# A two-layer hybrid encoder: weights' low halves by an accumulating DMA, a spread final norm, and work moved from VectorE and GpSimd

## Chip, cores and metric

One core of a Trainium2 chip runs the kernel. The metric is the device time of one execution in microseconds. Engines are named as in the profile: PE is TensorE's matmul (PEld its weight load), DVE VectorE, ACT ScalarE, POOL GpSimd, and SP is SyncE, which here only issues DMAs.

## What is computed

Two layers over 1024 tokens of width 1024, float32 throughout:

```python
u = rmsnorm(h, ln_mix[i]) @ w_in[i]
(c_q, c_kv, k_rope, gate_a, gq, gk, gv, lr_f, lr_b, gate_g) = split_cols(u, IN_SPLITS)
y_mla = mla_branch(c_q, c_kv, k_rope, positions, ...) * silu(gate_a)
y_gla = gla_branch(gq, gk, gv, lr_f, lr_b, ...) * silu(gate_g)
h = h + concatenate([y_mla, y_gla], axis=-1) @ w_out[i]
h = h + sigmoid(rmsnorm(h, ple_norm[i]) @ w_ple_gate[i]) * (p[i] @ w_ple_proj[i])
# after both layers: rmsnorm(h, final_norm)
```

`mla_branch` norms the latents c_q and c_kv, projects them to four heads' queries, keys and values, rotates a 64-wide shared key and part of the queries by position, and does dense softmax attention. `gla_branch` is a gated linear attention, four heads, run forward and backward in chunks of 64 tokens, with a norm per head.

## The kernel before

The activations lie transposed: features on the 128 partitions, 1024 tokens along the free dimension. Precision comes from splitting: a float32 value is a rounded high half and a low half (the rest), and a product is three matmuls, high x high, low x high, high x low (`mm3`, L156 to 163). Weights are loaded in pieces of 128 partitions x 512 columns or less by `load_split` (L135): SP issues the load into `wr` (two buffers), ACT copies it rounded to `wh` (L141), POOL subtracts for `wl` (L142); `wh` and `wl` have five buffers each. There are 192 such loads. Activations are split by ACT and DVE (`split`, L127).

Each layer starts with `rstd` (L165), which sums squares over partitions by a matmul with ones and finds the reciprocal root with small DVE operations. The norm's weights are folded into the split activations, and the factor r_x per token is applied to each projection as DVE evicts it from PSUM: `in_qk` (L323, two operations of 64 partitions and two DMAs that fill the other half of each tile), `in_v` (L332, factor per partition), `in_gate` (L354), `latent_tile` (L498). `latent_norm` (L505) takes a second root for the latents. `gla_decay`, `gla_state` and `gla_out` (L364, L405, L469) are the linear attention: chains of ACT exponentials, DVE scans and products, a recurrence of small DVE operations (L451), and short matmuls. `rotary_tables` (L241) computes sines and cosines once, on 128 partitions in four blocks of tokens, and writes them to DRAM; `rotary_key` (L574) works on 32 or 64 partitions. `score_rows`, `turn` and `attend` (L651, L677, L688) are the softmax attention; POOL scales the exponentials (L670).

The strings in `ORDER` (L52) list the steps of each layer in order, a letter for the step: K, Q, V and G the projections of the linear attention, Z, S, O its decay, state and output, C and D the latents, N and M their norms, A the attention's gates, R, X, E, T the rotary parts, H the query heads, k and v keys and values, s and b scores and attention, y and w the output projection. A planner, run at build time, then orders each engine's instructions by a simulated timeline; every engine and SP's queue take theirs strictly in that order. PSUM is two tags, `mm` and `aux`, of two tiles of two banks.

At the end the last gate (L800 to 847) goes over two blocks of tokens, 736 and 288 wide (`TAIL`). In each, for eight tiles: matmuls (L820), eviction (L823), sigmoid, product with `pj` on POOL (L828, the last two of block two on DVE), sum (L830), squares (L834, L836). After the eight, `rstd` and the final scaling, four tiles on POOL (L838 and L843, `POOL_END`) and four on DVE (L845), and the stores (L847).

## Time and profile before

| | us |
|---|---|
| median of three runs | 1482.35 (1480.93 to 1482.83) |
| the profiled execution | 1483.45 |
| its span, first to last instruction | 1481.7 |
| PE busy | 1387.9 (94%) |
| DVE busy | 929.8 (63%) |
| ACT busy | 625.7 (42%) |
| POOL busy | 573.4 (39%) |
| mean granted TensorE clock | 0.975 |

Busy time is the time in which an engine executes; its complement is waiting. The page's shares are means over stages that differ, so the stages are read by stretches: 56 to 400 us is the input projections and linear attention of layer 0, 400 to 680 its softmax attention and output projection, up to 775 its gate; 775 to 1095 and 1095 to 1370 are the like stages of layer 1, and the rest is the last gate and the final norm. The HBM reads come to 82.34 MB. The granted clock is 1 for 2.4 GHz and 0.5 for 1.2 GHz.

### The profile page before, as it was taken

What the parts mean: (1) busy time and instruction counts of PE and PEld (TensorE: products, weight loads), DVE (VectorE), ACT (ScalarE), POOL (GpSimd) and SP (SyncE); (2) the same over time, 40 slices, a digit from 0 to 9 for tenths busy, and PEclk for the clock granted to TensorE, in tenths of its full rate; (3) what the DMA queues carried; (4) which work ended last, traced back from release to release, by engine and by line L of the source; (5) the groups of instructions that cost most, each with busy time, mean ns of one, the idle gap of its engine ahead of it and who ended that gap; (6) DMA issues with size and microseconds to landing.
All of it is one profiled execution on the core that took longest, in us unless ns stands there. A gap on an engine that the chain in (4) does not pass through costs nothing. (4 is left out here: it accounts for less than half of the span.)

```text
span 1481.7 us, 20880 instructions
## 1 busy us (share of the span) xinstructions
PE 1387.9 (94%) x8404; PEld 1173.7 (79%) x8404; DVE 929.8 (63%) x1244; ACT 625.7 (42%) x828; POOL 573.4 (39%) x334
## 2 busy tenths in 40 slices
PE   8999899889889999999999989989989999999994
PEld 6799678678678888878889877768777888878994
DVE  2687856688655645465557878676755664447548
ACT  6454364443344534343444444623333543235331
POOL 4542332321264545223452323222334645412564
PEclk9999999999999999999999999999999999999997
DMA  8321213112501031112432121111350021211333
GB/s 293 116 74 51 62 66 144 33 51 81 157 27 57 15 100 50 64 43 86 152 134 65 37 72 51 36 54 37 121 143 29 29 71 50 71 45 55 124 103 122
DMA packets 51296, 117.51 MB, mean 79 GB/s; under 512 B 6592, under 2 KB 11584, under 8 KB 51200
## 3 DMA queue, kind: packets, MB, share of 16 engines
q1 hardware_dynamic: 51200, 116.19, 23.9%
q8 instruction: 66, 1.08, 0.3%
q14 instruction: 30, 0.25, 0.1%
HBM read 82.34 MB, written 25.43 MB: 73 GB/s over the span
## 5 line engine op out<-in xcount | busy, mean ns | idle before, releaser
L142 POOL TENSOR_TENSOR wl<-wr,wh 128x512 fp32r<-128x512 f32 (+2 forms) x184 | 270.3, 1472 | 690.0 <-ACT wh L141 615.8
L141 ACT ACTIVATE wh<-wr 128x512 fp32r<-128x512 f32 (+2 forms) x184 | 111.4, 610 | 336.9 <-PE ps L162 217.4
L670 POOL TENSOR_SCALAR sc<-sc,sums 128x1024 f32<-128x1024 f32 x64 | 181.9, 2851 | 91.4 <-DVE sums L669 76.8
L129 DVE TENSOR_TENSOR el<-ps,eh 128x1024 fp32r<-128x1024 f32 x64 | 78.0, 1221 | 47.2 <-ACT eh L128 46.4
L668 ACT ACTIVATE sc<-ps,top 128x1024 f32<-128x1024 f32 x64 | 71.4, 1116 | 82.5 <-DVE top L666 78.5
L162 PE MATMUL ps<-xh,wh 128*128 128x512 f32 x288 | 93.7, 406 | 12.2 <-DVE gate L357 5.9
L451 DVE SCALAR_TENSOR_TENSOR s<-s,last 64x128 f32<-64x128 f32 x208 | 84.6, 407 | 32.6 <-ACT s L104 25.7
L665 DVE TENSOR_REDUCE top<-ps 128x1 f32<-128x1024 f32 x64 | 78.2, 1223 | 39.8 <-PE ps L662 39.7
L162 PE MATMUL ps<-x0h,wh 128*128 128x512 f32 x288 | 93.1, 405 | 7.3 <-DVE gate L357 3.8
L162 PE MATMUL ps<-xh,wl 128*128 128x512 f32 x288 | 92.5, 400 | 0.0
L162 PE MATMUL ps<-x0h,wl 128*128 128x512 f32 x288 | 92.2, 400 | 0.0
L162 PE MATMUL ps<-xl,wh 128*128 128x512 f32 x288 | 91.7, 398 | 0.0
L162 PE MATMUL ps<-x0l,wh 128*128 128x512 f32 x288 | 91.5, 399 | 0.0
L162 PE MATMUL ps<-yh,wh 128*128 128x512 f32 x256 | 80.7, 392 | 0.9 <-DVE h L722 0.9
L162 PE MATMUL ps<-yl,wh 128*128 128x512 f32 x256 | 79.5, 390 | 0.0
L162 PE MATMUL ps<-yh,wl 128*128 128x512 f32 x256 | 79.3, 390 | 0.0
L128 ACT ACTIVATE eh<-ps 128x1024 fp32r<-128x1024 f32 x64 | 65.3, 1022 | 31.7 <-PE ps L683 30.1
L162 PEld LDWEIGHTS ps<-xh,wh 128*128 128x128 f32 x288 | 55.3, 195 | 25.3 <-DVE gate L357 6.4
L162 PEld LDWEIGHTS ps<-x0h,wh 128*128 128x128 f32 x288 | 55.2, 194 | 19.9 <-DVE gate L357 4.3
L683 PE MATMUL ps<-ident,sc 128*128 128x128 f32 x512 | 66.2, 273 | 4.6 <-DVE ql L129 3.0
L683 PEld LDWEIGHTS ps<-ident,sc 128*128 128x128 f32 x512 | 59.2, 140 | 13.0 <-DVE ql L129 3.5
L162 PEld LDWEIGHTS ps<-x0h,wl 128*128 128x128 f32 x288 | 55.8, 194 | 12.2
(251 smaller groups left out, 3499.3 us busy)
## 6 DMA issues: line engine op xcount, KB each, us to landing
wr<-in_w_in SPq DMA_DIRECT2D x88, 256.0 KB, 2.6
wr<-in_w_gate SPq DMA_DIRECT2D x40, 256.0 KB, 2.6
projd<-po SPq DMA_DIRECT2D x16, 512.0 KB, 3.7
wr<-in_w_out SPq DMA_DIRECT2D x32, 256.0 KB, 2.6
xraw<-in_xT SPq DMA_DIRECT2D x8, 512.0 KB, 4.8
gqk<-gqk SPq DMA_DIRECT2D x16, 256.0 KB, 3.0
ygd<-o SPq DMA_DIRECT2D x8, 512.0 KB, 2.6
gad<-gate SPq DMA_DIRECT2D x8, 512.0 KB, 3.0
```

What stands on the lines that cost most here:

```text
L128: nc.scalar.activation(hi, src, AF.Copy)
L129: nc.vector.tensor_tensor(lo, src, hi.bitcast(F32), op=ALU.subtract)
L141: nc.scalar.activation(hi[:, :n], raw[:, :n], AF.Copy)
L142: on("wlo").tensor_tensor(lo[:, :n], raw[:, :n], hi[:, :n].bitcast(F32), op=ALU.subtract)
L162: nc.tensor.matmul(ps[:, c, :], lhsT=a, rhs=b[:, c * HC:(c + 1) * HC], start=(i == 0 and j == 0), stop=(i == n - 1 and j == 2))
L451: nc.vector.scalar_tensor_tensor(state(n)[rows], state(m)[rows], alpha[rows, m:m + 1], state(n)[rows], op0=ALU.mult, op1=ALU.add)
L665: nc.vector.tensor_reduce(m, flat(ps), axis=AX.X, op=ALU.max, negate=True)
L668: nc.scalar.activation(e, flat(ps), AF.Exp, bias=m, scale=SCALE, accum_out=sums[:, b:b + 1])
L670: nc.gpsimd.tensor_scalar(e, e, sums[:, b:b + 1], None, op0=ALU.mult)
L683: nc.tensor.transpose(out=ps[:, j, b * P:(b + 1) * P], in_=e[:, kt], identity=ident)
```

## The change

All of it is made together:

- `load_split`: up to the step Q0 of layer 0 as before (eight loads). Later ones: ACT writes the negative rounded copy into `wl`, and a DMA issued on POOL reads the weights a second time from DRAM and adds them to it.
- `in_qk`: one DVE operation on 128 partitions into a tile of `st` (three buffers), and four DMAs that write both halves of both tiles.
- `in_v`: four ACT copies with a scale per partition in place of a DVE product, per half.
- `latent_tile`: ACT copies the PSUM tile unscaled and squares it from PSUM; `rstd` gets `base`, the mean square of x kept from the layer's first root (`ax`), so that the second root allows for the missing factor.
- `rotary_key`: on 128 partitions in four blocks of tokens. Eight DMAs lay out the key, six DVE operations of 256 columns rotate it, one split follows, eight DMAs write it to DRAM and four read it back in its two places. The tables stay in SBUF as `sc4`.
- The end: the product with `pj` is always DVE's. The scaling of the first block is spread, one tile per step, over the second block's steps, into tiles of `st`. `POOL_END` goes: DVE scales all tiles.

```diff
-POOL_END = (0, 3, 4, 6)
...
     other = [False]
+    first = [True]
     def pick(tag):
         return {"mm": "aux", "aux": "mm"}[tag] if other[0] else tag
...
         nc.vector.scalar_tensor_tensor(lo, src, g, hi.bitcast(F32), op0=ALU.mult, op1=ALU.subtract)
     def load_split(src, n, dst=None):
         raw = wp.tile([P, HC], F32, tag="wr", name="wr", bufs=BUFS[2])
         hi, lo = dst or (wp.tile([P, HC], F32R, tag=t, name=t, bufs=BUFS[3]) for t in ("wh", "wl"))
         with tc.high_priority():
             nc.sync.dma_start(raw[:, :n], src)
         nc.scalar.activation(hi[:, :n], raw[:, :n], AF.Copy)
-        on("wlo").tensor_tensor(lo[:, :n], raw[:, :n], hi[:, :n].bitcast(F32), op=ALU.subtract)
+        if first[0]:
+            nc.gpsimd.tensor_tensor(lo[:, :n], raw[:, :n], hi[:, :n].bitcast(F32), op=ALU.subtract)
+        else:
+            nc.scalar.activation(lo[:, :n], raw[:, :n], AF.Copy, scale=-1.0)
+            nc.gpsimd.dma_start(lo[:, :n], src, accum_op=ALU.add)
         return hi, lo
     def load_w8(src, keep=False):
...
                     nc.tensor.matmul(ps[:, c, :], lhsT=a, rhs=b[:, c * HC:(c + 1) * HC],
                                      start=(i == 0 and j == 0), stop=(i == n - 1 and j == 2))
-    def rstd(acc, width, n=S, tmp=st, res=mt, col=None):
+    def rstd(acc, width, n=S, tmp=st, res=mt, col=None, ax=None, base=None):
         if isinstance(acc, tuple):
             mat, parts = ones_r.bitcast(F32), acc
...
         y = cp.tile([P, 32], F32, tag="nwy", name="nwy", bufs=2)[:, :nb]
         t = cp.tile([P, 32], F32, tag="nwt", name="nwt", bufs=2)[:, :nb]
-        nc.vector.tensor_scalar(a, r[:, :n].rearrange("p (b i) -> p b i", i=32)[:, :, 0], 0.5 / width, 0.5 * EPS,
-                                op0=ALU.mult, op1=ALU.add)
+        nc.vector.tensor_scalar(a, r[:, :n].rearrange("p (b i) -> p b i", i=32)[:, :, 0], 0.5 / width,
+                                0.0 if base is not None else 0.5 * EPS, op0=ALU.mult, op1=ALU.add)
+        if base is not None:
+            nc.vector.scalar_tensor_tensor(a, base, EPS, a, op0=ALU.mult, op1=ALU.add)
+        if ax is not None:
+            nc.vector.tensor_copy(ax, a)
         nc.vector.tensor_scalar(y.bitcast(I32), a.bitcast(I32), 1, None, op0=ALU.arith_shift_right)
         nc.vector.tensor_scalar(y.bitcast(I32), y.bitcast(I32), -1.0, float(0x5F3759DF - 2 ** 22 - 2 ** 31),
                                 op0=ALU.mult, op1=ALU.add)
...
     h1d = dram([8, P, S], "h1d")
     cosd = dram([32, S], "cosd")
     sind = dram([32, S], "sind")
+    krd = dram([DEPTH, 2, 2, 32, S], "krd")
     def ple_projection(i):
         ops = []
...
                 copy("ple", o, flat(ps))
                 nc.sync.dma_start(projd[i][g * 2 + c], o)
+    sc4 = cp.tile([P, 2, S // 4], F32, name="sc4")
     def rotary_tables():
         n = S // 4
         work = mt(name="rot")
-        kk, ang, *rs = (work[:, i * n:(i + 1) * n] for i in range(4))
+        kk, ang = (work[:, i * n:(i + 1) * n] for i in range(2))
+        rs = sc4[:, 1], sc4[:, 0]
         posi = kk.bitcast(I32)
         for b in range(4):
             nc.sync.dma_start(posi[b * 32:(b + 1) * 32], pos[:, b * n:(b + 1) * n].to_broadcast((32, n)))
...
         rc = cp.tile([P, 8], F32, tag="rc", name="rc", bufs=2)
-        r_x = rstd(sq.acc, D, col=rc)
+        ax = cp.tile([P, 32], F32, tag="ax", name="ax", bufs=2)
+        r_x = rstd(sq.acc, D, col=rc, ax=ax)
         afb = mt(name="afb").rearrange("p (d t c) -> p d t c", d=2, c=CH)
         nc.gpsimd.memset(afb, 0.0)
...
             ps = flat(in_tile(t + j, tag))
             pair = (mt(name="gqk0"), mt(name="gqk1"))
-            for o, own, other in ((pair[0], slice(0, CH), slice(CH, P)), (pair[1], slice(CH, P), slice(0, CH))):
-                nc.vector.scalar_tensor_tensor(o[own], ps[own], scale, r_x[own], op0=ALU.mult, op1=ALU.mult)
-                nc.sync.dma_start(o[other], o[own])
+            both = st(name="gqk")
+            nc.vector.scalar_tensor_tensor(both, ps, scale, r_x, op0=ALU.mult, op1=ALU.mult)
+            halves = (slice(0, CH), slice(CH, P))
+            for o, own in zip(pair, halves):
+                for half in halves:
+                    nc.sync.dma_start(o[half], both[own])
             return pair
         def in_v(pair):
...
             res = []
             for half in range(2):
                 v = mt(name="gv").rearrange("p (t c) -> p t c", c=2 * P)
-                nc.vector.tensor_tensor(v, ps[half], rc[:, half * 4:half * 4 + 4].unsqueeze(2).to_broadcast((P, 4, 2 * P)),
-                                        op=ALU.mult)
+                for t in range(4):
+                    nc.scalar.activation(v[:, t], ps[half][:, t], AF.Copy, scale=rc[:, half * 4 + t:half * 4 + t + 1])
                 res.append(v)
             return [[res[t // 4][:, t % 4, h * P:(h + 1) * P] for t in range(8)] for h in range(2)]
...
         def latent_tile(t, s2, tile=mt):
             ps = in_tile(t)
             o = tile(name="craw")
-            nc.vector.tensor_tensor(o, flat(ps), r_x, op=ALU.mult)
-            s2.add(o)
+            nc.scalar.activation(o, flat(ps), AF.Copy)
+            s2.add(flat(ps))
             return o
         def latent_norm(raws, s2, off, width):
-            r = rstd(s2.acc, width)
+            r = rstd(s2.acc, width, base=ax)
             res = []
             for j, raw in enumerate(raws):
                 nc.vector.scalar_tensor_tensor(raw, raw, gv(off, j), r, op0=ALU.mult, op1=ALU.mult)
...
         def rotary_key():
-            cos, sin = xx[2:]
-            t1, t2 = mt(name="t1"), mt(name="t2")
-            k1, k2 = slice(64, 96), slice(96, 128)
-            nc.vector.tensor_tensor(t1[0:32], small[k1], cos[k1], op=ALU.mult)
-            nc.vector.tensor_tensor(t2[0:32], small[k2], sin[k2], op=ALU.mult)
-            nc.vector.tensor_tensor(t1[32:64], small[k1], sin[k1], op=ALU.mult)
-            nc.vector.tensor_tensor(t2[32:64], small[k2], cos[k2], op=ALU.mult)
-            nc.vector.tensor_tensor(t1[0:32], t1[0:32], t2[0:32], op=ALU.subtract)
-            nc.vector.tensor_tensor(t1[32:64], t1[32:64], t2[32:64], op=ALU.add)
+            n = S // 4
+            work = mt(name="kr")
+            k1, k2, u1, u2 = (work[:, i * n:(i + 1) * n] for i in range(4))
+            rot = mt(name="krot")[:, :2 * n]
+            cos, sin = sc4[:, 0], sc4[:, 1]
+            for b in range(4):
+                for k, row in ((k1, 64), (k2, 96)):
+                    nc.sync.dma_start(k[b * 32:(b + 1) * 32], small[row:row + 32, b * n:(b + 1) * n])
+            for x1, x2, o, op in ((cos, sin, rot[:, :n], ALU.subtract), (sin, cos, rot[:, n:], ALU.add)):
+                nc.vector.tensor_tensor(u1, k1, x1, op=ALU.mult)
+                nc.vector.tensor_tensor(u2, k2, x2, op=ALU.mult)
+                nc.vector.tensor_tensor(o, u1, u2, op=op)
+            parts = mt(F32R, "krp").rearrange("p (h c) -> p h c", h=2)
+            split(parts[:, 0], parts[:, 1], rot)
             ks, kl = mt(F32R, "ks"), mt(F32R, "kl")
-            nc.scalar.activation(ks[0:64], t1[0:64], AF.Copy)
-            nc.scalar.activation(ks[64:128], t1[0:64], AF.Copy)
-            for half in (slice(0, 64), slice(64, 128)):
-                nc.vector.tensor_tensor(kl[half], t1[0:64], ks[0:64].bitcast(F32), op=ALU.subtract)
+            for i, t in enumerate((ks, kl)):
+                for b in range(4):
+                    nc.sync.dma_start(krd[L, i, :, :, b * n:(b + 1) * n].rearrange("j f n -> f j n"),
+                                      parts[b * 32:(b + 1) * 32, i].bitcast(F32).rearrange("p (j n) -> p j n", j=2))
+                for half in (slice(0, 64), slice(64, 128)):
+                    nc.sync.dma_start(t[half].bitcast(F32), krd[L, i].rearrange("j f n -> (j f) n"))
             ksl.extend((ks, kl))
         def q_head(h):
...
             u = int(w[1])
             other[0] = w.endswith("+")
             h, c = divmod(u, 2)
+            if w == "Q0":
+                first[0] = False
             if w[0].isupper():
                 step(w[0], u)
             elif w[0] == "k":
...
                 xs.append((hi, lo))
         else:
-            kept = {}
+            kept, later = {}, []
+            def finish(t, w, r, o=None):
+                hw = hs[t][:, w]
+                o = hw if o is None else o[:, :w.stop - w.start]
+                nc.vector.scalar_tensor_tensor(o, hw, vec[:, V_FIN + t:V_FIN + t + 1], r, op0=ALU.mult, op1=ALU.mult)
+                nc.sync.dma_start(outT[t][:, w], o)
             for w in TAIL:
                 n = w.stop - w.start
                 k = -(-n // HC)
...
                     nc.scalar.activation(g, g, AF.Sigmoid)
                     pj = mt(name="pj")[:, :n]
                     nc.sync.dma_start(pj, projd[L][t][:, w])
-                    eng = nc.vector if last_block and at > 5 else nc.gpsimd
-                    eng.tensor_tensor(g, g, pj, op=ALU.mult)
+                    nc.vector.tensor_tensor(g, g, pj, op=ALU.mult)
                     hw = hs[t][:, w]
                     nc.vector.tensor_tensor(hw, hw, g, op=ALU.add)
                     if at == 0:
                         nc.scalar.activation(acc, hw, AF.Square)
                     else:
                         nc.scalar.activation(g, hw, AF.Square)
-                        if at < 7:
+                        if at < 7 or not last_block:
                             nc.vector.tensor_tensor(acc, acc, g, op=ALU.add)
-                    if at in POOL_END:
-                        nc.vector.tensor_scalar(hw, hw, vec[:, V_FIN + t:V_FIN + t + 1], None, op0=ALU.mult)
-                r_f = rstd((acc, g), D, n=n)
-                for at, t in enumerate(todo):
-                    hw = hs[t][:, w]
-                    if at in POOL_END:
-                        nc.gpsimd.tensor_tensor(hw, hw, r_f[:, :n], op=ALU.mult)
-                    else:
-                        nc.vector.scalar_tensor_tensor(hw, hw, vec[:, V_FIN + t:V_FIN + t + 1], r_f[:, :n],
-                                                       op0=ALU.mult, op1=ALU.mult)
-                    nc.sync.dma_start(outT[t][:, w], hw)
+                    if later:
+                        finish(*later.pop(0), st(name="fin"))
+                if last_block:
+                    r = rstd((acc, g), D, n=n)
+                    for t in todo:
+                        finish(t, w, r[:, :n])
+                else:
+                    r = rstd(acc, D, n=n)
+                    later = [(t, w, r[:, :n]) for t in todo]
```

## Rows read from the trace of the kernel before

**Rows 1.** The page's table of busy time, share of the span, instructions

```profile
PE 1387.9 (94%) x8404; PEld 1173.7 (79%) x8404; DVE 929.8 (63%) x1244; ACT 625.7 (42%) x828; POOL 573.4 (39%) x334
```

**Rows 2.** Stretches: busy us and (x instructions) per engine, granted clock, DMA share, GB/s

```profile
56.00:400.00 344.00, 319.29 (x2336) 269.10 (x2337) 249.61 (x360) 150.50 (x202) 102.92 (x68) 0.96 0.24 78
...
775.00:1095.00 320.00, 297.99 (x2262) 252.67 (x2261) 234.42 (x341) 134.12 (x182) 93.76 (x65) 0.97 0.21 65
...
1459.60:1481.70 22.10, 3.46 (x11) 1.65 (x9) 16.01 (x40) 4.20 (x10) 5.39 (x6) 0.58 0.34 123
```

**Rows 3.** Waits of PE, 56 to 400 us: total us, times, longest

```profile
PE ps L176 <- ACT sqh L128: 6.9, 2, 4.8
PE ps L162 <- DVE gate L357: 5.3, 2, 3.8
PE ps L477 <- DVE s L451: 4.8, 1, 4.8
```

**Rows 4.** Waits of PE, 775 to 1095 us

```profile
PE ps L162 <- DVE gate L357: 7.2, 2, 5.9
...
PE ps L162 <- DVE gqk L328: 1.0, 1, 1.0
```

**Rows 5.** Groups of POOL by line, shape: xcount, busy us, mean ns

```profile
L142 POOL TENSOR_TENSOR wl<-wr,wh 128x512 fp32r<-128x512 f32 x164 | 250.0, 1528 | 604.5 <-ACT wh L141 537.8 <-issue 66.6
```

**Rows 6.** Groups of ACT by line and shape

```profile
L141 ACT ACTIVATE wh<-wr 128x512 fp32r<-128x512 f32 x164 | 101.8, 626 | 291.9 <-PE ps L162 185.4 <-issue 57.0 <-DMA wr<-in_w_in 13.0
...
L128 ACT ACTIVATE eh<-ps 128x1024 fp32r<-128x1024 f32 x64 | 65.3, 1022 | 31.7 <-PE ps L683 30.1 <-PE ps L162 1.4
```

**Rows 7.** Groups of DVE by line and shape

```profile
L328 DVE SCALAR_TENSOR_TENSOR gqk<-ps,rstd 64x1024 f32<-64x1024 f32 x16 | 19.5, 1221 | 5.7 <-PE ps L162 5.3
...
L398 DVE TENSOR_TENSOR d<-d,gqk 128x1024 f32<-128x1024 f32 x8 | 15.5, 1932 | 8.2 <-ACT d L396 8.2
...
L501 DVE TENSOR_TENSOR craw<-ps,rstd 128x1024 f32<-128x1024 f32 x10 | 12.1, 1218 | 0.2
...
L401 DVE TENSOR_TENSOR qi<-qi,gqk 128x1024 f32<-128x1024 f32 x8 | 9.8, 1225 | 6.7 <-ACT qi L395 6.7
...
L349 DVE TENSOR_TENSOR gv<-ps,rc 128x1024 f32<-128x1024 f32 x8 | 9.6, 1214 | 0.0
...
L589 DVE TENSOR_TENSOR kl<-t,ks 64x1024 fp32r<-64x1024 f32 x4 | 6.2, 1540 | 1.2 <-ACT ks L586 1.1
...
L579 DVE TENSOR_TENSOR t<-small,cos 32x1024 f32<-32x1024 f32 x2 | 2.4, 1214 | 1.9 <-DMA cos<-cosd 1.9
...
L838 DVE TENSOR_SCALAR h<-h,vec 128x736 f32<-128x736 f32 x4 | 2.4, 596 | 0.9 <-ACT acc L832 0.9
```

**Rows 8.** Timeline of DVE at the end

```profile
1450.57 9.70 DVE L845 SCALAR_TENSOR_TENSOR h<-h,vec,rstd 128x736 f32<-128x736 f32 x4
...
1466.85 0.44 DVE L823 TENSOR_TENSOR gt<-ps,rstd 128x288 f32<-128x288 f32 x1
...
1474.20 4.04 DVE L845 SCALAR_TENSOR_TENSOR h<-h,vec,rstd 128x288 f32<-128x288 f32 x4
```

**Rows 9.** Tile wl by stretches: PE, PEld and POOL instructions that touch it

```profile
56.00:400.00 344.00, 140.14 (x454) 88.09 (x454) 81.10 (x51) 0.96 0.24 78
...
775.00:1095.00 320.00, 132.51 (x430) 82.86 (x430) 70.31 (x48) 0.97 0.21 65
```

**Rows 10.** DMA issues: line, queue, xcount, KB each, median us to landing

```profile
wr<-in_w_in SPq DMA_DIRECT2D x88, 256.0 KB, 2.6
...
xraw<-in_xT SPq DMA_DIRECT2D x8, 512.0 KB, 4.8
```

**Rows 11.** Timeline of PE inside one projection: start us, us

```profile
1076.52 0.62 PE L162 MATMUL ps<-xl,wh 128*128 128x512 f32 x2
...
1082.00 0.61 PE L162 MATMUL ps<-xl,wh 128*128 128x512 f32 x2
```

**Rows 12.** Timeline of SP's queue, cosine loads of layer 1

```profile
1051.67 1.81 SPq L571 DMA_DIRECT2D cos<-cosd  x4
```

More of the change, by code (lines that the diff above doesn't have):

```diff
@@ L53 @@
          "Q0 K0 Z0 V0 S0 Z1 V1 S1 Q1 K1 Z2 G0 O0 S2 G1 Z3 G2+ C0 O1 D0 O2 S3 G3 C1 N0 D1 D2+ O3 M0 X0 A0 A1 E0 A2 k0 y2 H0 A3 T0 s0 v0 H3 k1+ s1 H1 b0 H2 s2 k2 b1 s3 y0 k3+ b2 v1 s4 y3 y1 b3 s5 b4 w0 w1+ s6 w2+ b5 w3 s7 w4 b6 w5+ s8 w6+ w7 b7")
-ENG = dict(at="V", qi="V", qb="P", og="P", gate="P", sq="V", wlo="P", kT="A", put="A", o="A", ple="A", hadd="V")
+ENG = dict(at="V", qi="V", qb="P", og="P", gate="P", sq="V", kT="A", put="A", o="A", ple="A", hadd="V")
 TCKW = {"schedule_with_timeline_sim": True}
```

## The prediction

> **What bounds the kernel now.** I read the table of the page first: PE is busy 1387.9 us of a span of 1481.7 [rows 1]. So the room is the 94 us in which PE stands still, plus what it loses at the lower clock. A table by stretches [rows 2] says where: 24.7 us idle in 56 to 400 us and 22.0 us in 775 to 1095 us (the projections and the gated linear attention of the two layers), and 18.6 us after the last projection matmul, 1459.6 us to the end. The first two stretches run at a mean granted clock of 0.96 and 0.97, and PE falls to its lower level, 1.2 GHz, after its longest idle gaps. What that costs is at most 0.04 x 319 + 0.03 x 298 = 21.7 us. The other stretches hold some 28 us of idle time, in small pieces.
>
> Next I read whom PE waited for in the two stretches [rows 3, 4]. Released by DVE: 18.1 us in 56 to 400 (seven rows; gate and s are the largest) and 18.6 us in 775 to 1095 (seven rows; gate and gqk are shown). Released by ACT: 8.3 and 2.6 us, sqh first. No row names POOL. DVE is also the busiest of the other engines there: 249.6 of 344 us and 234.4 of 320 [rows 2]. So the kernel is bound by PE, and where PE stands still DVE is usually late.
>
> **The lows of the weights.** Removed: POOL's subtraction for 184 of 192 loads (the eight before Q0 of layer 0 stay). It takes 1.53 us [rows 5]. Added: a second ACT copy, 0.63 us [rows 6], and one DMA issued on POOL, 184 x 256 KB or less.
> - POOL gives up about 270 us. PE never waited for it, so the gain is indirect. POOL's two-input operations slow DVE's: d x k takes 1.93 us where the like product with qi takes 1.23 [rows 7], and at the end DVE's final scaling takes 2.4 us for 736 columns beside POOL, where 1.23 us for 1024 columns scales to 0.89 [rows 7, 8]. Over DVE's groups in the two stretches I estimate 37 us of such excess (5.7 of it in those eight products). POOL's subtractions are 81.1 and 70.3 us there, of 102.9 and 93.8 us of POOL [rows 2, 9], so I take three quarters: DVE gets back 14 us per layer. Bounds: 0 and 18.
> - ACT pays 51 x 0.63 = 32 us and 48 x 0.63 = 30 us in the two stretches [rows 6, 9]. Elsewhere 85 more copies lie beside PE.
> - The low half now comes by a DMA that no row shows. Nearest: a plain load of the same size lands in 2.6 us, the slowest big load of the start in 4.8 [rows 10]. It moves the same bytes with a second read, so I take 5 us, 2.6 to 10. The cover is the five buffer pairs: a load feeds 24 matmuls, 5.48 us (twelve rows of two; the first of them and the one after the last are shown) [rows 11], so a load is made about four loads ahead, some 22 us. Even 10 us is hidden, and I charge nothing. Without the cover it would be a few us for each load.
> - POOL's issue of such a DMA has no row. From below it is SP's 0.45 us per issue [rows 12], from above the subtraction it replaces, 1.53 us. I take 1 us, off the path. Queued behind a waiting issue on POOL are the products of the output and the softmax scaling, as they are behind the subtraction now.
> - The raw buffer comes free after ACT's second copy, earlier than after POOL's subtraction, so SP's loads and what stands behind them in SP's queue start a little earlier. I count nothing.
>
> Against this part speaks the Trainium skill (SBUF — State Buffer, the paragraph on the "DVE blocks DMA" trap): while DVE runs a copy-like operation in its faster two-port mode, POOL cannot write the descriptors of a DMA it issues. No run here shows such a DMA. The trace shows DVE operations at twice the usual speed, but short ones: 736 columns in 0.60 us [rows 7]. By the page a DMA would start up to that much later, still inside the lead, so it would leave the sum as it is.
>
> **DVE's shorter list.** q and k: eight 128-row operations replace 16 half-height ones of 1.22 us, -9.8 us. Values: eight of 1.21 leave DVE, -9.6, and become 32 ACT copies of 256 columns, about 0.43 each by 0.63 for 512, +13.8. Latents: ten of 1.22 leave, -12.1, and become ACT copies of 1.02, +10.2; the PSUM bank is then held by two ACT reads, which matters only if ACT is late. Key: six operations of 1.2 to 1.6 us and two of 1.54, per layer, go (21.3 us over both) for six of 256 columns, about 0.35, and one of 512, about 0.7; over both layers 5.6, so -15.7; ACT saves 3. The new copies of the norm's base cost +1.2. DVE: -46 us, 23 per layer [rows 6, 7].
> Queues: SP gets 28 more issues per layer (8 for q and k, 20 for the key), 0.45 us each [rows 12], 13 us. The key's three hops in a row take 3 x 2.6 us and 5 us of work. The key is wanted only at the first scores; two gate tiles, a query head and the first keys come between, four projections of 4 to 11 us. Weight loads behind those hops have the 22 us lead. Charged: 0.
>
> **From work to time.** DVE's load in the two stretches falls by 23 + 14 = 37 us of 250 and of 234, some 15%. The 36.7 us that PE waits for DVE go by between nothing (if they are latencies of one chain) and all. I take a third, -13, since the waits are queueing behind a DVE at 73%, with chains in between. The clock returns a like share of 21.7: -7.5 (0 to -21.7). ACT gets about 86 - 3 us more in these stretches (62 + 13.8 + 10.2, less the key), going from 44% and 42% to some 56%. PE's 10.9 us of waits for ACT grow: +4 (0 to +40).
>
> **The end.** The last matmul ends at 1459.8, but its eviction starts at 1466.85, because the four final scalings of the first columns hold DVE for 9.7 us [rows 8]. From that eviction to the last scalings it is 7.35 us, and from the end of those (1474.20 + 4.04) to the end of the span 3.46 us. With DVE free at 1459.9 and eight scalings of 0.37, it would end at 1459.9 + 7.35 + 3.0 + 3.46 = 1473.7: -8. If the eight scalings of the first columns (8 x 0.89 = 7.1 us) and the products that come over from POOL (8 x 0.4) still stand in the queue, nothing is won. I take -4.
>
> Sum: -13 - 7.5 + 4 - 4 = -20.5 against the profiled execution (1483.45 us, the span and 1.75 around it). It stands 1.1 us above the median of 1482.35, so from the median: 1461.9, rounded to 1462.
>
> **Rivals.**
> - ACT takes DVE's place (slower). Place: the two stretches, where ACT is served in order and already stands with a weight copy at its head until PE frees the buffer; the exponentials and evictions queue behind two copies instead of one. Price: the part of the 83 us that lands ahead of a PE wait. It decides from 28.5 us (13 + 7.5 + 4, and the 4 of the sum), a third of it. At half: 41.5 - 24.5 = +17, 1499 us. For: 8.3 us of PE's waits are for ACT. Against: ACT remains under 60%. Chance 0.16.
> - The low halves come late. By rows: if landing plus issue exceeds the 22 us lead, each load costs a fifth of the excess, so 30 us would cost 184 x 8 / 5 = 294 us, 1776 us. It would take DVE's two-input work, and not the short fast operations alone, to hold up POOL's issues. That is the trap of the page named above, taken further than it goes. Against it: the 2.6 us row. Chance 0.04.
> - The waits are chains, not queues: DVE is relieved but PE's order and its waits stay. Then only the end gives: 1482.35 - 4 = 1478, or no change if ACT takes that too. Chance 0.16, half of it within the bound.
> - Contention was the main thing: DVE gets back all, and two thirds of waits and clock go: 36.7 x 2/3 + 21.7 x 2/3 + 6 = 45 less 4, 1441 us. It is the good end of my own case.
>
> **How the numbers follow.** My case has 0.64 (1441 to 1475), the chains 0.16, ACT 0.16, late lows 0.04. A measurement of this kernel can tell about 0.2%, 3 us, from no change. Faster: 0.64 + 0.08 = 0.72. Same 0.08. Slower 0.20. The range from 1440 to 1488 leaves out the upper part of the ACT case, the late lows and the best end of mine.
>
> **What would show it.** Right: DVE busy in 56 to 400 down from 250 to about 213 us and ACT up to about 195; the product d x k at 1.2 us; PE's waits for DVE there at 12 us; the clock at 0.97 or more; the last eviction less than 4 us after the last matmul. Wrong: PE waiting at its projections for the accumulating DMA; PE waits for ACT above 30 us; the span between the last matmul and the end still at 22 us; PE's waits for DVE unchanged though DVE's busy time fell.

## The result and the profile after

The changed kernel takes 1473.88 us (median of five runs, 1472.4 to 1477.46) against 1482.83 us for the kernel before, run beside it: ratio 0.9941 [0.9928, 0.9954]. It is 9 us faster, where 20.5 were forecast. The profiled execution spans 1470.7 us, 11.0 less than before [rows 1].

The page, busy times and the two DMA queues (packets, MB, share of 16 engines):

```profile
PE 1379.4 (94%) x8400; PEld 1168.9 (79%) x8400; DVE 819.2 (56%) x1238; ACT 737.0 (50%) x1053; POOL 427.4 (29%) x312
...
q1 hardware_dynamic: 55168, 124.05, 27.9%
q0 software_dynamic: 26496, 46.41, 18.9%
```

POOL is down from 573 to 427 us, DVE from 930 to 819, ACT up from 626 to 737 [rows 1]; q0 is the accumulating traffic on POOL's queue.

To find where the span changed, both traces are cut at the same points of PE's work: layer 0's and layer 1's first score matmul, the start of layer 1, the end of its output projection, the last gate's last matmul. The same cuts for four experiments, which are described below, stand beside them (us between cuts, each cut to within 0.8 us; the first 56 us are left out):

| stretch | before | after | e13 | e4 | e12 | e7 |
|---|---|---|---|---|---|---|
| 56 us to layer 0's first scores | 342.0 | 325.0 | 326.8 | 325.6 | 352.3 | 326.1 |
| to the start of layer 1 | 360.0 | 359.0 | 360.2 | 358.4 | 361.7 | 359.9 |
| to layer 1's first scores | 331.0 | 331.0 | 319.7 | 322.3 | 335.5 | 340.0 |
| to the end of its output projection | 275.0 | 276.6 | 276.0 | 275.9 | 275.8 | 277.9 |
| to the last gate's last matmul | 96.5 | 102.4 | 98.7 | 100.8 | 102.3 | 95.5 |
| to the end | 21.2 | 20.7 | 20.8 | 21.9 | 25.4 | 21.0 |

Layer 0 gains 17 us, the like stretch of layer 1 nothing, and the last gate loses 5.9. In after, layer 1's stretch holds 28 matmuls more than before: the whole of the first values' projection now runs ahead of the first scores, where before a part of it ran behind them. So layer 1's two stretches, to its first scores and on to the end of its output projection, are best read together: 606.0 us before, 607.6 after, 595.7 in e13. Three questions follow: what gives the 17, what takes the same gain from layer 1, and what slows the gate.

The kernel before by such cuts (columns as in [rows 2]):

```profile
56.00:398.00 342.00, 317.29 (x2327) 267.45 (x2328) 248.38 (x359) 149.45 (x200) 102.18 (x67) 0.96 0.24 77
758.00:1089.00 331.00, 309.65 (x2298) 261.58 (x2297) 242.55 (x348) 141.03 (x189) 99.02 (x67) 0.97 0.20 66
1364.00:1460.50 96.50, 95.17 (x593) 93.42 (x591) 59.30 (x71) 31.83 (x46) 55.41 (x36) 1.00 0.33 109
```

The kernel after, with the stretches of [rows 2] among them:

```profile
56.00:381.00 325.00, 310.01 (x2327) 262.89 (x2327) 199.48 (x348) 181.71 (x268) 63.36 (x66) 0.98 0.54 131
56.00:400.00 344.00, 326.66 (x2398) 276.00 (x2398) 210.22 (x364) 191.95 (x283) 76.30 (x72) 0.99 0.54 133
740.00:1071.00 331.00, 310.88 (x2326) 263.86 (x2325) 196.28 (x333) 171.84 (x257) 66.78 (x68) 0.97 0.49 115
775.00:1095.00 320.00, 292.78 (x2224) 247.10 (x2223) 188.51 (x318) 165.30 (x249) 67.03 (x63) 0.96 0.48 112
1347.60:1450.00 102.40, 96.07 (x588) 94.85 (x586) 54.25 (x88) 43.79 (x70) 17.29 (x20) 0.97 0.64 154
```

By the fixed stretches DVE is busy 210.2 and 188.5 us, ACT 192.0 and 165.3, and the clock is 0.99 and 0.96. The fixed stretch of 56 to 400 us now holds some attention, though. For equal PE work in layer 0 (2327 matmuls in either trace) DVE falls from 248.4 to 199.5, and in layer 1, with the 28 matmuls more, from 242.6 to 196.3. In layer 0 PE's idle time falls from 24.7 to 15.0 us and its busy time by 7.3 (the clock goes from 0.96 to 0.98); in layer 1 idle stays near 20 us.

Waits of PE over the whole span of after (they answer to [rows 3, 4]: total, times, longest):

```profile
PE ps L670 <- DVE ql L129: 11.1, 2, 7.1
...
PE ps L857 <- DMA wl<-in_w_gate: 5.9, 1, 5.9
PE ps L167 <- DVE afb L482: 5.8, 1, 5.8
...
PE ps L167 <- DVE gate L376: 5.2, 3, 4.6
...
PE ps L690 <- DMA qs<-rl: 5.0, 1, 5.0
PE ps L182 <- ACT sqh L128: 4.6, 3, 2.1
```

Two rows wait on DMAs that hardly mattered before (0.7 us for `qs`): `wl` in the last gate and the rotated query `qs` in layer 1.

Groups of DVE after ([rows 7] show d x k before), then the same recurrence in the kernel before:

```profile
L470 DVE SCALAR_TENSOR_TENSOR s<-s,last 64x128 f32<-64x128 f32 x208 | 78.2, 376 | 37.9 <-ACT s L102 30.8
...
L417 DVE TENSOR_TENSOR d<-d,gqk 128x1024 f32<-128x1024 f32 x8 | 12.4, 1549 | 18.2 <-ACT d L415 18.2
```

```profile
L451 DVE SCALAR_TENSOR_TENSOR s<-s,last 64x128 f32<-64x128 f32 x208 | 84.6, 407 | 32.6 <-ACT s L104 25.7
```

The recurrence, 208 operations with no change of code, went from 407 to 376 ns. d x k fell from 1.93 to 1.55 us, not to 1.23. Six of the eight products now take 1.21 to 1.23 us, four of them while POOL issues a DMA; the other two take 2.48 and 2.58 us beside POOL's product `b`, which is still there.

Groups of ACT and of POOL after [rows 5, 6], and the page's DMA issues after [rows 10]:

```profile
L146 ACT ACTIVATE wl<-wr 128x512 fp32r<-128x512 f32 x156 | 97.9, 628 | 269.3 <-PE ps L167 244.4 <-PE ps L362 11.6 <-PE ps L857 7.9
...
L369 ACT ACTIVATE gv<-ps,rc 128x256 f32<-128x256 f32 x32 | 12.7, 481 | 2.6 <-PE ps L362 2.6
...
L521 ACT ACTIVATE craw<-ps 128x1024 f32<-128x1024 f32 x10 | 10.1, 1009 | 0.0
```

```profile
L147 POOL DMA_DIRECT2D wl<-in_w_in x84 | 72.6, 870 | 354.0 <-ACT wl L146 327.5 <-ACT wh L142 13.2 <-ACT wzt L317 6.3
```

```profile
wr<-in_w_in SPq DMA_DIRECT2D x88, 256.0 KB, 3.3
wl<-in_w_in POOLq DMA_DIRECT2D x84, 256.0 KB, 4.8
...
wl<-in_w_gate POOLq DMA_DIRECT2D x32, 256.0 KB, 4.8
```

An accumulating DMA lands in 4.8 us (the medians of both groups shown) and takes POOL 0.87 us to issue; plain loads now take 3.3 us where they took 2.6.

### The profile page after: what moved, and what is told of

It reads as the page before. It is cut to its first block, busy times and chain, and to the rows that moved or that the text cites. A ratio compares the mean times of both kernels' runs of the same rounds, so it can differ in the third digit from the quotient of the medians.

```text
span 1470.7 us, 21244 instructions
## 1 busy us (share of the span) xinstructions
PE 1379.4 (94%) x8400; PEld 1168.9 (79%) x8400; DVE 819.2 (56%) x1238; ACT 737.0 (50%) x1053; POOL 427.4 (29%) x312
## 3 DMA queue, kind: packets, MB, share of 16 engines
q1 hardware_dynamic: 55168, 124.05, 27.9%
q0 software_dynamic: 26496, 46.41, 18.9%
## 5 line engine op out<-in xcount | busy, mean ns | idle before, releaser
L146 ACT ACTIVATE wl<-wr 128x512 fp32r<-128x512 f32 (+2 forms) x176 | 107.5, 611 | 296.8 <-PE ps L167 271.8
L147 POOL DMA_DIRECT2D wl<-in_w_in x84 | 72.6, 870 | 354.0 <-ACT wl L146 327.5
L470 DVE SCALAR_TENSOR_TENSOR s<-s,last 64x128 f32<-64x128 f32 x208 | 78.2, 376 | 37.9 <-ACT s L102 30.8
L167 PE MATMUL ps<-x0h,wh 128*128 128x512 f32 x288 | 89.9, 393 | 1.5 <-ACT sq L219 1.1
L147 POOL DMA_DIRECT2D wl<-in_w_out x32 | 27.9, 872 | 169.5 <-ACT wl L146 168.9
L167 PEld LDWEIGHTS ps<-xh,wh 128*128 128x128 f32 x288 | 54.7, 193 | 22.8 <-DVE afb L482 6.2
L711 PEld LDWEIGHTS ps<-ident,sc 128*128 128x128 f32 x512 | 59.2, 140 | 15.7 <-DVE ql L129 3.6
```

Source lines behind the costliest of these rows:

```text
L146: nc.scalar.activation(lo[:, :n], raw[:, :n], AF.Copy, scale=-1.0)
L147: nc.gpsimd.dma_start(lo[:, :n], src, accum_op=ALU.add)
L167: nc.tensor.matmul(ps[:, c, :], lhsT=a, rhs=b[:, c * HC:(c + 1) * HC], start=(i == 0 and j == 0), stop=(i == n - 1 and j == 2))
L470: nc.vector.scalar_tensor_tensor(state(n)[rows], state(m)[rows], alpha[rows, m:m + 1], state(n)[rows], op0=ALU.mult, op1=ALU.add)
L711: nc.tensor.transpose(out=ps[:, j, b * P:(b + 1) * P], in_=e[:, kt], identity=ident)
```

## Experiments

Twelve kernels ran, four to eleven times each, with the kernel before beside them in three jobs (medians 1484.83, 1484.43 and 1484.67 us). Beside the whole change the kernel before had 1482.83 us, some 2 us less. So an experiment's raw median understates what it gains over the whole change (1473.88 us, ratio 0.9941) by about that much, and the ratios are the surer comparison.

### What takes layer 1's gain: the key's queue

In after, ACT's timeline ahead of layer 1's attention (start, us, idle before and its releaser), then SP's queue and PE's timeline in the same stretch:

```profile
1047.68 0.42 ACT L142 ACTIVATE wh<-wr 128x256 fp32r<-128x256 f32 x1
1058.38 1.06 ACT L128 ACTIVATE yh<-yraw 128x1024 fp32r<-128x1024 f32 x1 [10.28 <-DMA yraw<-ygd]
...
1060.17 1.00 ACT L128 ACTIVATE qh<-ps 128x1024 fp32r<-128x1024 f32 x1
```

```profile
1048.73 1.84 SPq L617 DMA_DIRECT2D kl<-krd  x2
...
1051.83 1.03 SPq L781 DMA_DIRECT2D yraw<-ygd  x1
```

```profile
1062.49 0.51 PE L670 MATMUL ps<-wh,ch 128*128 128x256 f32 x1 [4.00 <-DVE ql L129]
...
1077.66 0.76 PE L690 MATMUL ps<-ks,qs 128*128 128x512 f32 x1 [5.01 <-DMA qs<-rl]
```

ACT takes its instructions in the order given. At 1048.1 us its next is `yh`, a step of the output projection that nobody needs yet, and it waits 10.28 us for `yraw`. SP issues that load at 1051.83, behind the key's writes and reads (the last of them shown). The query head `qh` stands behind `yh`; so `ql` is late, and PE waits 4.0 us for it at 1062.49 and 5.0 for `qs` at 1077.66.

**e1_key_old**: the change with the old `rotary_key`.

```diff
-nc.sync.dma_start(k[b * 32:(b + 1) * 32], small[row:row + 32, b * n:(b + 1) * n])
...
+nc.vector.tensor_tensor(t1[0:32], small[k1], cos[k1], op=ALU.mult)
...
```

> The changed kernel with the key's rotation of before (eight DVE operations on 32 or 64 partitions and two ACT copies, no DMAs). Orders differ only around it. Theory K (20 more issues on SP and their transfers make the gate values' load yraw late, ACT stands 10.3 us with its copy at the head, and layer 1's first scores start late): the wait of ACT for yraw goes below 3 us and PE's waits between 1060 and 1085 us fall from 11 to 5 us or less; 1464 to 1469. Rival D (DVE's 15 us of longer work is what counts): PE's waits for DVE grow by 3 us or more, 1474 to 1480.

1460.63 us, ratio 0.9833 [0.9815, 0.9850], better than either expectation. Layer 1's first scores come 319 us after its start (after: 331), `yraw` is issued at 1039.47, and ACT waits 1.8 us for it. The new key costs 13 us by the medians as it stands (16 by the ratios), though it takes work from DVE.

**e10_y_later**: the key stays; in the order of layer 1 the step y2, which loads `yraw`, moves behind v0. No work changes.

```diff
-... A2 k0 y2 H0 A3 T0 s0 v0 H3 ...
+... A2 k0 H0 A3 T0 s0 v0 y2 H3 ...
```

> The changed kernel (1473.9 us) with the step y2 of layer 1 (load and split of a gated head from the linear attention) moved from behind k0 to behind v0; the key's DMAs stay. Layer 0, where no y step stands there, showed no loss by the key. Theory Y (the key's loss is ACT standing 10.3 us with the copy of yraw at its head, behind the key's DMAs): layer 1's first scores come 7 to 12 us earlier, 1462 to 1468. Rival Q (it is SP's issues and the slower landings, which make the queries' own DMAs late as well): 1471 to 1476.

1463.29 us, ratio 0.9859 [0.9842, 0.9876], as Theory Y expected; layer 1's first scores come 320 us after its start. ACT's timeline of this kernel, at the same place:

```profile
1048.82 1.01 ACT L128 ACTIVATE qh<-ps 128x1024 fp32r<-128x1024 f32 x1
```

`qh` runs 11 us earlier, with all the key's DMAs still there. So the loss is not the DMAs' time as such but a wait at the head of ACT's queue for a load that they push back. Layer 0 has no y step at this place and loses nothing.

### What slows the last gate: the low half's latency

PE's timeline in the second block of columns of after, then ACT's and POOL's rows for the weight it waits for:

```profile
1418.86 0.29 PE L857 MATMUL ps<-hl,wh 128*128 128x288 f32 x1
1419.49 0.40 PE L857 MATMUL ps<-hh,wh 128*128 128x288 f32 x1 [0.35 <-ACT wh L142]
1425.81 0.61 PE L857 MATMUL ps<-hh,wl 128*128 128x288 f32 x1 [5.92 <-DMA wl<-in_w_gate]
```

```profile
1417.58 0.82 ACT L861 ACTIVATE gt<-gt 128x736 f32<-128x736 f32 x1 [1.89 <-DVE gt L860]
1418.31 0.61 ACT L146 ACTIVATE wl<-wr 128x512 fp32r<-128x512 f32 x1
```

```profile
1419.21 0.87 POOL L147 DMA_DIRECT2D wl<-in_w_gate  x1 [11.29 <-ACT wl L146]
```

Neighbouring matmuls of 288 columns start 0.133 us apart here, so a load that serves twelve of them is used up in 1.6 us, and the five buffer pairs hold 8 us of PE's work, not 22. In ACT's order the copy stands behind a sigmoid that had waited for DVE; it ends at 1418.92, POOL issues at 1419.21, and PE can go on at 1425.81. The matmuls behind the stall start 0.24 us apart (granted clock 0.50, the 1.2 GHz level, from 1426.3 to 1430.9 us; 1.00 ahead of the stall), and the first block's `rstd` goes on only at 1433.59.

**e2_gate_pool**: the change, but POOL subtracts again for the loads of the last gate (one line, `first[0] = True` ahead of the loop over `TAIL`).

> The changed kernel (1473.9 us), but the last layer's gate (from line 857) takes its low halves by POOL's subtraction again. PE's order is the same up to there. Theory A (short lead: a load of the second block feeds only 12 matmuls, 1.6 us, so five buffers are 8 us ahead, about the copy, issue and landing together): PE's wait of 5.9 us for the accumulating DMA in the second block goes, the last matmul comes 6 to 8 us earlier, DVE's root for the first block too, and the time is 1466 to 1469. Rival B (the end is set by DVE's own list of scalings): PE's wait goes but the last eviction stays where it is, 1472 to 1475. Rival C (POOL's subtractions again slow DVE in the first block): 1474 to 1478.

1471.01 us, ratio 0.9900 [0.9882, 0.9918]: PE's wait for `wl` in the gate is gone. The time lies between the expectations of Theory A and Rival B.

**e8_interleave**: the change, with the second block's tiles ordered so that loads alternate with tiles whose weights are kept.

```diff
-todo = [t for t in range(8) if t not in kept] + list(kept)
+todo = [0, 4, 1, 5, 2, 6, 3, 7] if kept else list(range(8))
```

> The changed kernel, with the second block's tiles in the order 0, 4, 1, 5, 2, 6, 3, 7, so that a tile whose weights are kept comes between two that are loaded. The accumulating DMA stays. Theory A: the lead in time doubles to some 13 to 16 us, PE's wait for the low half is under 1 us, 1466 to 1469. Rival (the accumulating DMA is late whatever the order, as landings are slow there): the wait stays 4 to 6 us, 1472 to 1475.

1471.01 us, ratio 0.9910 [0.9897, 0.9924], between the two expectations as well; the same wait is gone and the stage takes 96.0 us, as before (96.5). By the profile the stage had lost 6 us. The raw medians of e2 and e8 show 3 of them, their ratios against that of the whole change 6 and 5.

### Both at once

**e9_key_old_inter** is e1 with e8's order.

> The changed kernel with the key's rotation of before (1460.6 us) and the second block's tiles in the order 0, 4, 1, 5, 2, 6, 3, 7. Both losses that were found are taken out. If they add: PE's wait of 3.5 us for the low half in the last gate goes, 1455 to 1459. Rival (the wait covers DVE's list, which then ends no earlier): 1460 to 1462.

1460.25 us, ratio 0.9840 [0.9827, 0.9853]: no different from e1, as the rival said. In e1 PE's wait for `wl` was 3.5 us, and taking it away gave nothing that could be measured.

**e13_both_orders** is the whole change with e10's and e8's orders. Nothing is added or left out.

> The whole change, with two orders altered and no work added or removed: layer 1's step y2 behind v0, so that ACT does not stand for yraw behind the key's DMAs, and the last gate's second block in the order 0, 4, 1, 5, 2, 6, 3, 7, so that PE does not wait for the accumulating DMA there. Theory Z (the two charges that were set to nothing, the key's queue and the latency in the last gate, are what is missing against the forecast of 1462): 1458 to 1462 us, ratio 0.982 to 0.985, and PE waits neither for wl nor for qs by DMA. Rival (they overlap with another wait that takes their place, as the clock or DVE at the end): 1463 to 1466 us, ratio 0.985 to 0.988, as the order of y2 alone gives.

1460.66 us, ratio 0.9838 [0.9823, 0.9852]. Waits of PE over its whole span, the first rows:

```profile
PE ps L182 <- ACT sqh L128: 7.6, 4, 3.5
PE ps L670 <- DVE ql L129: 7.0, 1, 7.0
```

No wait on a DMA is above 1.4 us, and the total is within 1.4 us of the forecast of 1462. By the kernel before beside it the gain is 24.0 us, where 20.5 were forecast. Against e10 the second order adds 2.6 us, with overlapping intervals; what shows for certain is the sum. This kernel, e1 and e9 are the fastest of the study, and the three can't be told apart.

### What the gain comes from: POOL's two-input work

**e4_lows_only**: the kernel before with the accumulating DMA alone (the edit of `load_split` and of Q0).

> The kernel before (1482.8 us) with the accumulating DMA alone. Theory A with the short lead: DVE gets back some 30 us of contention in all, of which PE's stretches gain 4 to 8 us, the last gate loses 6 to 8; 1479 to 1486. Rival (contention was the main thing): DVE's product d x k at 1.25 us, PE's idle time in the two stretches down by 15 us, 1470 to 1476. Rival (ACT becomes late): PE's waits for ACT above 25 us, 1488 or more.

1465.85 us, ratio 0.9869 [0.9854, 0.9884]: this part by itself beats the whole change, and every expectation (the best was 1470 to 1476). Its stretches between the cuts:

```profile
56.00:381.60 325.60, 311.72 (x2326) 263.52 (x2325) 220.85 (x360) 172.85 (x248) 63.44 (x65) 0.98 0.52 119
740.00:1062.30 322.30, 303.99 (x2296) 257.51 (x2295) 221.02 (x347) 163.66 (x237) 67.37 (x67) 0.99 0.46 105
```

DVE's list is that of before (360 and 347 operations), but it is busy 220.9 and 221.0 us in place of 248.4 and 242.6. That is 27.5 and 21.5 us. Over the two layers the scans along 1024 tokens give 9.3 us of it (45.9 to 36.6), the recurrence 7.6 (84.6 to 77.0, 370 ns each), the products `gqk<-d,ref` 5.9 (15.7 to 9.8) and d x k only 1.7 (1.73 us each, against the 1.25 expected).

**e12_paced**: e4 with POOL doing an operation of the same size for every load, whose result nobody reads.

```diff
+nc.gpsimd.tensor_tensor(scr[:, :n], hi[:, :n].bitcast(F32), hi[:, :n].bitcast(F32), op=ALU.subtract)
 nc.gpsimd.dma_start(lo[:, :n], src, accum_op=ALU.add)
```

> The kernel before with the accumulating DMA, and beside it POOL subtracts wh from itself into a scratch tile, once per load, as soon as ACT's wh copy is there: the same size and about the same moment as the old subtraction, but nothing waits for its result and it holds no buffer longer. The output is unchanged. Theory P (the gain of the DMA is DVE freed from POOL's two-input work): DVE busy goes back to 246 to 252 us in 56 to 400 us and to 231 to 237 us in 775 to 1095 us, and the ratio to the kernel before is 0.993 to 1.008. Rival B (the gain is that the raw buffer comes free earlier, or that the low half no longer depends on POOL's turn): DVE busy stays near 231 and 215, and the ratio stays below 0.990.

1508.33 us, ratio 1.0164 [1.0151, 1.0177]. Its stretches:

```profile
56.00:408.30 352.30, 320.75 (x2328) 270.31 (x2329) 251.81 (x360) 174.52 (x250) 122.71 (x117) 0.95 0.48 111
770.00:1105.50 335.50, 311.43 (x2295) 262.95 (x2294) 241.22 (x346) 163.20 (x236) 122.25 (x116) 0.96 0.44 100
```

DVE is back at 251.8 and 241.2 us with the same list: POOL's operations make DVE slower, whatever they are for, and Rival B falls. e12 differs from e4 by POOL's operations alone, and with them PE's waits for DVE go from 12.1 to 23.6 us in layer 0's stretch and from 12.6 to 19.0 in layer 1's. The time overshoots the kernel before by 24 us, outside Theory P's range; by the cuts of its profiled execution, which is 27 us longer, 10 us of that lie in layer 0's stretch, 4.5 in layer 1's and 10 in the last gate and the end. What e12 has more than that kernel is POOL's issues beside its subtractions (122.7 us busy in layer 0's stretch against 102.2) and ACT's second copies (174.5 against 149.5). In layer 0's stretch PE's waits for DVE are 23.6 us in place of 18.1 and those for ACT no longer (8.1 and 8.3), but which of the two additions costs the time was not tried. So e12 settles where DVE's time comes from, and not how many us the relief is worth.

DVE's and POOL's timelines of e12 show the effect in one place:

```profile
167.48 6.26 DVE L456 SCALAR_TENSOR_TENSOR s<-s,last 64x128 f32<-64x128 f32 x8 [0.44 <-ACT s L104]
...
174.15 3.01 DVE L456 SCALAR_TENSOR_TENSOR s<-s,last 64x128 f32<-64x128 f32 x8
```

```profile
167.12 2.40 POOL L500 TENSOR_TENSOR o<-o,gate 128x1024 f32<-128x1024 f32 x1 [1.17 <-DVE o L499]
171.63 0.87 POOL L147 DMA_DIRECT2D wl<-in_w_in  x1 [2.12 <-ACT wl L146]
172.24 1.34 POOL L147 TENSOR_TENSOR scr<-wh 128x512 f32<-128x512 f32 x1
```

Eight operations of the recurrence take 6.26 us beside POOL's product and scratch operation and 3.01 us without. The difference, 3.25 us, is nearly the time for which those two run beside them (2.04 + 1.34 us). The Trainium skill (SBUF — State Buffer, "SBUF: two separate sides") says that the two engines share one pair of ports, that it is locked for a whole instruction, also between a DVE operation with two inputs in SBUF and a POOL operation that reads SBUF, and that the loser waits. By that rule the eight would be held up for all of the overlap; the trace agrees, with 3.25 of 3.38 us.

**e11_pool_back** was an earlier form: a subtraction of scratch from itself after each DMA, which waits for nothing.

> The kernel before with the accumulating DMA alone (1465.9 us), and behind each of these DMAs a subtraction of the same size and kind on POOL, on a scratch tile that nothing else uses. It puts POOL's load back without its hold on the raw buffer and without its place before PE. Theory P (POOL's two-input work slows DVE's, and that made PE wait): 1478 to 1486, DVE's busy time from 56 to 400 us back at 245 to 250. Rival R (the raw buffer's earlier release, and so SP's queue, made the gain): 1464 to 1469.

1561.99 us, ratio 1.0524 [1.0507, 1.0541], far above either expectation, and not usable for the size: with nothing to wait for, the extra operations crowded into layer 0 (POOL had 216 instructions there in 56 to 400 us, against 68), and 78 us of the 82 by which its span is longer lie ahead of its first scores. e12 was made for that reason.

**e5_short_dve**: the kernel before with q and k in one operation, values on ACT and the unscaled latents; lows, key and end as before.

> The kernel before (1483 to 1485 us) with the shorter list of DVE alone: one operation for q and k, values scaled by ACT, unscaled latents. Lows by POOL, the key and the end as before. Theory S (substitutes: in layer 0 the low halves alone already took away the waits of PE that DVE's lateness made; the shorter list does the same work on the same waits): it gains by itself, 1470 to 1477, and layer 0's first scores come 8 to 17 us earlier than before. Rival N (these operations never stood before a wait of PE): 1480 to 1487, the first scores within 4 us of before.

1478.69 us, ratio 0.9961 [0.9948, 0.9974], between the two expectations. Layer 0's first scores come 10.8 us earlier, as Theory S said, but layer 1 gives most of it back. What is left on DVE also gets slower: the recurrence takes 429 ns in place of 407 and d x k 2.13 us in place of 1.93, with POOL's subtractions as before.

**e7_lows_pool**: the whole change with POOL's subtraction for all loads.

> The whole change without the accumulating DMA: POOL subtracts for all 192 loads, as before. Theory P: without it little is left. DVE busy 56 to 400 us is 228 to 238 us (231 less what DVE's shorter list took off, plus 18 of contention), the ratio to the kernel before is 0.994 to 1.004, so slower than the whole change or equal to it. Rival S (the shorter DVE list does the same as the DMA, and the key's queue costs as much in either): within 3 us of the whole change, 1471 to 1477 us, with PE's wait for the DMA in the last gate gone.

1477.81 us, ratio 0.9954 [0.9941, 0.9966]; against the whole change the intervals overlap. The ratio and DVE's 234.4 us in 56 to 400 us are as Theory P expected, and the time is 0.8 us above Rival S's range, so e7 does not decide between them. In the whole change as it stands, what the DMA adds to the shorter list is thus not shown to be more than nothing. e7's stretches:

```profile
56.00:382.10 326.10, 312.48 (x2328) 263.86 (x2327) 225.84 (x349) 155.65 (x218) 97.72 (x67) 0.98 0.31 93
742.00:1082.00 340.00, 310.74 (x2303) 263.07 (x2302) 220.88 (x334) 148.23 (x208) 97.70 (x67) 0.96 0.26 76
```

Layer 0 gains as much as with the DMA (326.1 us), with DVE at 225.8 in place of 199.5; layer 1 loses 9 us, although DVE is 22 us below before. So the two ways to relieve DVE do not add up in layer 0: the shorter list brings 11 us (e5) or 16 (e7, with the new key), the DMA 16 (e4), both 17. What layer 1 loses without the DMA is only partly read: by its waits PE stands for ACT's `sqh` and `wh` there (7.8 and 3.1 us up to 1015 us). No run takes that apart.

### The end alone

**e6_end_only**: the kernel before with the new end.

> The kernel before with the new end alone: the products with pj on DVE, the first block's scalings spread over the second block's steps, all scalings on DVE. Forecast: -4 us (0 to -8). Theory E (DVE is still the bound of the end: POOL's eight products and four scalings come over to it, so what is won at the final scalings is paid in the second block): within 2 us of the kernel before, ratio 0.9985 to 1.0015, and the time from the last matmul of the gate to the end of the span is 20 to 22 us as before (21.2). Rival F (the end gives its gain when the gate does not wait for the DMA): ratio 0.995 to 0.998, and 13 to 18 us from that matmul to the end.

1482.95 us, ratio 0.9990 [0.9980, 0.9999]: 1.7 us faster by the medians, between nothing and 3 by the interval, as Theory E expected. DVE's timeline in e6, then in after:

```profile
1466.47 0.45 DVE L830 TENSOR_TENSOR gt<-ps,rstd 128x288 f32<-128x288 f32 x1
```

```profile
1433.59 0.95 DVE L185 STREAM_TRANSPOSE rstd<-ps 128x736 f32<-128x736 f32 x1 [7.97 <-PE ps L182]
...
1455.63 0.45 DVE L860 TENSOR_TENSOR gt<-ps,rstd 128x288 f32<-128x288 f32 x1
...
1463.72 3.52 DVE L834 SCALAR_TENSOR_TENSOR h<-h,vec,rstd 128x288 f32<-128x288 f32 x8
```

In e6 the last gate matmul ends at 1460.7 and its eviction starts 5.8 us later (before: 6.4 us, 1466.85 against 1460.47). In after it is 5.7. From the last matmul to that eviction DVE never stands idle for more than 0.2 us: products, sums and the first block's scalings fill the time. From that eviction to the final scalings it takes 8.1 us, where it took 7.35.

## Why the prediction was right and wrong

**Right: the sign and what bounds the kernel.** PE waits for a DVE that POOL slows, and relief of DVE comes back as PE time. e4 shows that the relief pays, e12 that it is relief from POOL's operations and not the buffers. Of the signs named as right, DVE at 210 us, ACT at 192, PE's waits for DVE at 11.1 us in layer 0 and the clock at 0.99 came; d x k came in six of eight products, and the early last eviction did not.

**Right: the small prices.** Landing 4.8 us (taken: 5), issue 0.87 (1), second copy 0.63, value copies 0.48 (0.43), latents 1.01 (1.02).

**Wrong: "Charged: 0" for the queues of the shorter list.** This is the largest miss: 10 to 13 us by the medians, 12 to 16 by the ratios (e10, e1). The text counted 13 us of issues on SP and asked whether the key and the weight loads would be late. It did not go through what else stands in SP's queue behind the key: the load of `yraw`, and behind `yraw`'s use on ACT, the query head. The key's three hops were also longer, with median landings of 3.7, 2.1 and 4.9 to 5.1 us, 11 in all where 8 were taken.

**Wrong: "Even 10 us is hidden, and I charge nothing".** The lead of 22 us was worked out from one projection of 1024 columns and taken for all loads. In the last gate's second block it is 8 us, against 1.2 us of copies, 0.87 of issue and a landing of 4.8, which leaves some 1 us for ACT's order, and ACT was later than that. It cost 6 us of the stage, and 5 to 6 of the time by the ratios (e8, e2; 3 by the raw medians).

**Wrong: "I take -4" at the end.** Measured: -1.7, or between 0 and -3 (e6). The text named the condition itself: the first block's scalings and the products still stand in DVE's queue ahead of the last eviction, and so next to nothing is won. It also put the end of the last matmul 0.7 us too early (1459.8 for 1460.5).

**Under-sized: the contention, 14 us per layer with a bound of 18.** e4 shows 27.5 and 21.5. The estimate of 37 us in all names, inside the two stretches, only d x k, with 5.7 us; in e4 that product gives back 1.7, and the scans, the recurrence and the products with `ref` 22.8, with the rest spread over many rows. With the shorter list too, DVE falls by 49 and 46 us, not 37.

**Right by size, not as a rate: a third of the waits, and the clock.** Forecast -20.5 for both stretches. With the two orders changed (e13) they give, by the like cuts, 15.2 + 11.3 = 26.5 us, of which 15.4 are idle time and 11.1 PE's busy time (from 24.7 + 21.3 idle to 15.7 + 14.9). PE's waits for DVE there fall from 36.7 to 22.7 us, 14 where 13 were forecast; in the whole change they fall to 27.3. But in layer 0 DVE relieved by 22 us (e7), 27 (e4) or 49 (after) gives 16 to 17 alike, so the gain there does not grow with the relief, and a rate of a third of the waits is a lucky hit. Why it stops at 17 stays open.

**Wrong in sign: ACT's +4.** PE's waits for ACT in layer 1's stretch are 3.8 us in after (`sqh`; before 2.6), and in layer 0's they fall from 8.3 to below 4. In the whole change ACT's added copies, at 56 and 52% busy, cost nothing that shows; what ACT cost was the one wait at the head of its queue, for a load behind the key's DMAs. e7 and e12 show PE waiting for ACT, with POOL still at work.

**The sum, as measured in the profiled executions:** layer 0 -17.0, its attention -1.0, layer 1 0 and its attention +1.6 (together -10.3 with e13's orders), last gate +5.9, end -0.5: -11.0.

**The rivals.** ACT in DVE's place: no. Chains, not queues: no, by e4 and e12, though layer 0's limit of 17 us may be of that kind. Contention as the main thing: in part; DVE got back more than was taken, but the best kernels gain 24 us and not 41. Late lows: only in the last gate, by a short lead more than by a long landing (6.6 us from issue to PE's start there, median 4.8). The Trainium skill's trap (SBUF — State Buffer, the paragraph "DVE blocks DMA") was weighed there; a median landing of 4.8 us over 84 loads, with 0.87 us to issue, is far inside the lead of 22 us, but how much of it is such a delay no run here can tell. The row read there as "twice the usual speed" is 1.5 times: 0.60 us, where 736 columns scale to 0.89.

## What to carry to other kernels

A DMA that costs no engine time can still cost the time of whatever stands behind it in its queue: follow each queue past the moved step to the first instruction with a consumer, on the issuing queue and then on the engine that waits for the pushed-back load. A lead in buffers is worth as many microseconds as the consumer spends on them in that stage, so work it out for the stage with the smallest tiles. When a change has many parts, the gains need not add up while each part's cost stays: here one part alone (1465.9 us) beat all of them together (1473.9), and two changes of order brought the whole to 1460.7.

## What the runs showed of the hardware that was not expected

POOL's two-input operations cost DVE nearly their whole overlap (3.25 of 3.38 us in the place shown of e12), also for operations as small as 64 x 128 (0.38 us alone, 0.78 beside POOL). POOL's issue of a DMA does not: four products d x k of after overlap such an issue by 0.43 to 0.88 us and take 1.21 to 1.23 us. In this kernel the accumulating traffic takes more of the DMA engines per byte than plain traffic: 18.9% of the span for 46.41 MB against 27.9% for 124.05 MB, 1.8 times as much, and plain weight loads landed in 3.3 us in place of 2.6 beside it.
